# Attention in a two-stream encoder step: two PSUM banks used as halves, and a unit's output transposed two steps later

## The chip, the cores and the metric

The kernel runs on one core of one Trainium2 chip. The metric is the device time of one execution in microseconds. The core has five engines that run side by side, each its own queue in order: PE (TensorE, matrix products and transposes; its weight loads are listed as PEld), DVE (VectorE), ACT (ScalarE), POOL (GpSimd) and SP (SyncE, which here issues the DMAs). Products land in PSUM, which is eight banks of 128 partitions x 512 float32 values; DVE and ACT read them out from there into SBUF.

## The reference

One layer of an encoder is computed for 1024 prompt frames and for 64 new frames of a running stream that has a cache of 512 frames. All data are float32.

```python
z = einsum('btd,de->bte', x, w_in)      # one projection, its columns split among three head groups
# A: forgetting attention, 6 heads x 64, causal
s = q @ k.T / 8 + c_q - c_k              # c = cumsum(log f)
o_fox = softmax(where(kpos <= qpos, s, -1e30)) @ v
# B: chunked gating, 4 groups x 64: u * (tril(w_s) @ layer_norm(gelu(v)) + b_s) within 128 positions
# C: stick-breaking attention, 6 heads x 64, strictly causal
a = sigmoid(z) * prod over s < j < t of (1 - sigmoid(z_tj));  o_sb = a @ v
o = per-head RMSNorm([o_fox, o_sgu, o_sb]) * g_mix @ w_out
x = layer_norm(ALPHA * x + o);  x = layer_norm(ALPHA * x + square(relu(x @ w_up)) @ w_down)
```

The outputs are the new x of both streams and the new rows of keys, values, log forget gates and normalised gate rows.

## The kernel before

To keep float32 accuracy, an operand is split into a high and a low part, and a product is made of several passes over them (`PASSES`). A usual pair of instructions is thus an ACT copy that rounds to the high part and a DVE or POOL subtraction (`lo_sub`, line 98) that leaves the low part.

The kernel has three phases. Up to about 600 us: projections, attention and gating. Then, to about 700 us, the output projection ("mix") and the first LayerNorm. Then the MLP, whose products are on lines 1290 and 1748. Only the first phase is touched.

In the first phase two streams of work are written out one step at a time by a loop (lines 1092 to 1138): `fill()` makes the projections, whose products are on lines 360 and 501, in blocks of eight matmuls, and `attn()` does attention. The loop takes the next step from the stream that is behind by an estimate of its cost. This gives the order of the program. A planner then simulates the program on its own times and writes out each engine's queue; an instruction that comes later in the program can pass one whose inputs, in the simulation, are not ready. On the chip each queue runs in the written order.

Attention goes through six pairs of heads (three of A, then three of C). A pair has eight units and a sample unit. A unit is a block of 256 queries (u = 0 to 3) of one head (h = 0, 1). Its `a_steps` make two half rows of scores (line 559) and weights. Its `b_steps` use the weights in u + 2 steps: `tr` transposes up to four 128x128 blocks of them on PE (L607) into a bank "pt", from which ACT (L575) and DVE (L98) make the high and low part `pth`; `av` multiplies these with the values in four matmuls (L617 and L618 with the high part, L619 and L620 with the low part) into a bank "o", the sums over keys. In the last step ACT copies "o" to `osb` (L630), an SBUF tile with one buffer. The former unit's `c_step` then transposes `osb` on PE (L638, twice) into a bank "tr", DVE adds the two halves of the products into `ot` (L639), also one buffer, and after the second head of a block SP stores `ot` to HBM (L643). The sample unit makes its sums in "o" as well (L739, L743), and DVE takes them out straight into a new `ot` (L746), which has to wait for the store of the one before.

The bank "tr" has two other users: the keys of a projection are transposed there (`finish`, L484) and so are the cached keys of the sample (L676); both are taken out by `k_stack` with two ACT copies (L446) and two DVE subtractions.

PSUM is divided by tag: "acc", "s" and "pt" have two banks each, "o" and "tr" one each. A tile of "o" or "tr" is 256 columns wide, half of a bank, and each unit opens a new tile (`bufs=1`).

`attn()` interleaves the steps of the unit at hand (`b`) with the `a_steps` of the next (`nxt`), by turns, the next unit's first. A counter `k` counts the steps; after the second the pending `c_step` of the former unit is written out (line 1064). Where the next unit's queries are not projected yet, the unit at hand is first finished without counting.

## Time and profile before

| | |
|---|---|
| median of 3 runs | 1399.08 us (1395.83 to 1399.73) |
| profiled execution | 1399.96 us, its span 1398.2 us |
| mean granted TensorE clock | 0.983 |
| busy: PE, PEld, DVE, ACT, POOL | 1328.2, 1208.2, 1000.0, 720.2, 606.3 us |
| PE busy from 60 to 360 us, clock | 287.90 of 300 us, 0.99 |
| PE busy from 360 to 600 us, clock | 223.75 of 240 us, 0.95 |

In the profile a name such as `osbsb` is the tile's name without its numbers: "o" of a unit of pair "sb", and `osbsb` is also how `osb` of "sb" is shown; the line tells which is meant (L617 to L620 write the PSUM tile, L630 copies it into SBUF). `otpsb` is the tile in "tr". A row of a timeline has the start in us, the duration, the engine, line, operation, tile written <- tiles read, and in brackets how long the engine stood idle before it and for whom. A row of the waits has who waited for whom, the total in us, how often, and the longest.

### The profile page before, as it was taken

The page shows a single profiled execution, that of the slowest core. Times are in us where ns is not written, and L with a number is a line of the kernel's source. Part 1 is how long each engine was busy: PE and PEld are TensorE (multiplying, and loading weights), DVE is VectorE, ACT ScalarE, POOL GpSimd, SP SyncE. Part 2 cuts the span into 40 slices and gives each one's busy share as a digit, 9 for nine tenths or more (in the row PEclk, how much of TensorE's full clock was granted, in tenths as well). Part 3 has the DMA queues.
Part 4 walks back from the last instruction along what each step waited for, and adds up shares of the span by engine and source line. Part 5 has one row for each costly group of instructions (what it writes and reads, how often), then busy time and mean ns, then how long its engine had stood idle before and what let it go on. Part 6 is the DMA issues. An engine that isn't in the chain of part 4 may idle for free.

```text
span 1398.2 us, 24326 instructions
## 1 busy us (share of the span) xinstructions
PE 1328.2 (95%) x8827; PEld 1208.2 (86%) x8827; DVE 1000.0 (72%) x1795; ACT 720.2 (52%) x1561; POOL 606.3 (43%) x667
## 2 busy tenths in 40 slices
PE   7999999999898998999989999999998999999996
PEld 6899989999888987866889999999986788887875
DVE  3577666577788379787776687787668677767777
ACT  4366566566556366333432332322256677667675
POOL 3222222256665436755421222122156765565657
PEclk9999999999999999999999999999999999999999
DMA  7445564231403257432223444443468244444343
GB/s 219 91 130 157 156 203 122 65 80 43 106 16 72 64 161 252 150 112 68 76 85 118 167 140 131 155 140 122 169 232 309 91 169 141 145 136 154 99 135 128
DMA packets 159088, 185.64 MB, mean 133 GB/s; under 512 B 27756, under 2 KB 117164, under 8 KB 158968
## 3 DMA queue, kind: packets, MB, share of 16 engines
q1 hardware_dynamic: 158968, 184.08, 41.7%
q8 instruction: 70, 1.15, 0.3%
q14 instruction: 50, 0.41, 0.1%
HBM read 117.65 MB, written 60.10 MB: 127 GB/s over the span
## 4 chain that ended last, share of the span: by engine, by line
PE 65%; DVE 11%; DMA 8%; ACT 6%; POOL 5%; issue 4%; SPq 1%; DVEq 0%; ACTq 0%; POOLq 0%
PE zA L1290 9%; PE A L1748 8%; PE mx L249 7%; PE zD L1290 6%; PE kvsb L360 5%; PE D L1748 4%; PE zC L1290 3%; PE zB L1290 3%; PE kvfox L360 3%; PE B L1748 2%; DMA rwo<-w_out 2%; POOL wd L98 1%; PE qsb L501 1%; DVE snsb L543 1%; DMA xr<-x_prompt 1%
## 5 line engine op out<-in xcount | busy, mean ns | idle before, releaser
L98 POOL TENSOR_TENSOR wa<-wr,wa 128x512 fp32r<-128x512 f32 x42 | 62.8, 1521 | 227.0 <-ACT wa L1230 227.0
L98 POOL TENSOR_TENSOR wd<-rd,wd 128x512 fp32r<-128x512 f32 x77 | 100.3, 1314 | 107.9 <-ACT wd L1230 103.6
L249 PE MATMUL mx<-xT,oTb 128*128 128x512 f32 (+1 forms) x416 | 108.1, 412 | 1.0 <-ACT oTb L207 0.9
L1290 PE MATMUL zD<-xo,ws 128*128 128x288 f32 (+1 forms) x720 | 98.0, 289 | 1.9 <-DVE h4a L1454 1.6
L1290 PE MATMUL zA<-xo,ws 128*128 128x288 f32 (+1 forms) x720 | 98.0, 290 | 0.0
L249 PEld LDWEIGHTS mx<-xT,oTb 128*128 128x128 f32 (+1 forms) x416 | 78.7, 194 | 20.3 <-ACT oTb L207 1.4
L1290 PEld LDWEIGHTS zD<-xo,ws 128*128 128x128 f32 x720 | 93.6, 189 | 2.4 <-DVE h4a L1454 1.8
L1290 PEld LDWEIGHTS zA<-xo,ws 128*128 128x128 f32 x720 | 94.2, 190 | 0.0
L360 PE MATMUL kvfox<-wkvfox,xT 128*128 128x256 f32 (+3 forms) x624 | 90.2, 293 | 3.2 <-DVE fx L463 2.1
L1422 POOL TENSOR_TENSOR rd<-rd 128x512 f32<-128x512 f32 x56 | 79.3, 1417 | 29.3 <-DVE b L98 27.0
L545 POOL TENSOR_TENSOR sgsb<-sgsb,snsb 128x127 f32<-128x127 f32 (+7 forms) x48 | 58.4, 1217 | 75.8 <-DVE snsb L543 67.0
L360 PE MATMUL kvsb<-wkvsb,xT 128*128 128x256 f32 (+1 forms) x624 | 88.4, 287 | 0.0
L1230 ACT ACTIVATE wd<-rd 128x512 fp32r<-128x512 f32 x105 | 63.5, 623 | 45.1 <-POOL rd L1422 23.4
L1748 PE MATMUL A<-wd,wd 128*128 128x512 f32 x312 | 83.3, 396 | 3.3 <-DVE acc L1715 2.3
L360 PEld LDWEIGHTS kvfox<-wkvfox,xT 128*128 128x128 f32 (+1 forms) x624 | 81.3, 192 | 4.9 <-DVE fx L463 2.4
L543 DVE TENSOR_TENSOR_SCAN snsb<-snsb,one 128x128 f32<-128x128 f32 (+7 forms) x48 | 72.5, 1514 | 15.4 <-ACT snsb L542 14.7
L360 PEld LDWEIGHTS kvsb<-wkvsb,xT 128*128 128x128 f32 (+1 forms) x624 | 79.5, 187 | 0.2
L1301 ACT ACTIVATE sn<-zA 128x256 f32<-128x256 f32 (+1 forms) x80 | 30.9, 389 | 91.8 <-PE zA L1290 72.9
L1748 PEld LDWEIGHTS A<-wd,wd 128*128 128x128 f32 x312 | 58.1, 188 | 19.3 <-DVE acc L1715 3.6
L1748 PE MATMUL A<-wd,h4a 128*128 128x512 f32 x240 | 64.5, 394 | 0.6 <-DVE acc L1715 0.4
L1508 ACT ACTIVATE ws<-wr 128x1024 fp32r<-128x1024 f32 x28 | 29.0, 1056 | 57.4 <-DVE wr L1240 57.4
L1748 PEld LDWEIGHTS A<-wd,h4a 128*128 128x128 f32 x240 | 44.7, 188 | 12.2 <-ACT wd L1230 0.8
(548 smaller groups left out, 3754.5 us busy)
## 6 DMA issues: line engine op xcount, KB each, us to landing
h_dr<-hh SPq DMA_DIRECT2D x30, 512.0 KB, 3.2
rd<-w_down SPq DMA_DIRECT2D x30, 512.0 KB, 4.3
wr<-w_up SPq DMA_DIRECT2D x13, 1024.0 KB, 5.5
hr<-h_dr SPq DMA_DIRECT2D x31, 384.0 KB, 4.7
h_dr<-hh SPq DMA_DIRECT2D x30, 384.0 KB, 4.1
raw<-w_in SPq DMA_DIRECT2D x44, 256.0 KB, 3.4
wo_dr<-swo SPq DMA_DIRECT2D x32, 256.0 KB, 2.6
xT<-wo_dr SPq DMA_DIRECT2D x8, 1024.0 KB, 7.8
```

Of the source, the lines that this page charges most:

```text
L98: eng.tensor_tensor(out, src, hi.bitcast(F32), op=ALU.subtract)
L249: nc.tensor.matmul(acc[0:m], oT[:, k, hx, 0:m], wo[k // 4][hw][:, k % 4, cs], start=(i == 0), stop=(i == len(seq) - 1))
L360: nc.tensor.matmul(acc[0:n, c0:c0 + n1 - n0], xT[k // 4][:, k % 4, c:c + n], wt[:, k, hw, n0:n1], start=(i == 0), stop=(i == len(seq) - 1))
L501: nc.tensor.matmul(acc[:, 0:w], wq[:, k, hw, :], xT[k // 4][:, k % 4, c:c + w], start=(i == 0), stop=(i == len(seq) - 1))
L543: nc.vector.tensor_tensor_scan(g[:, 0:n][:, ::-1], g[:, 0:n][:, ::-1], one.broadcast_to([P, n]), 1.0, op0=ALU.mult, op1=ALU.bypass)
L545: nc.gpsimd.tensor_tensor(s[:, 0:n - 1], s[:, 0:n - 1], g[:, 1:n], op=ALU.mult)
L1230: nc.scalar.activation(hi, raw, AF.Copy)
L1290: nc.tensor.matmul(z, w[:, hw, k], xop(s, bo, hx)[:, k, :], start=(new and k == 0 and j == 0), stop=(k == 3 and j == 2), skip_group_check= ...
L1301: nc.scalar.activation(c, z, AF.Copy)
L1422: eng.tensor_tensor(r[:, o], r[:, x], r[:, y], op=ALU.subtract)
L1508: nc.scalar.activation(ws[:, 0, q, c], src[:, q], AF.Copy)
L1748: nc.tensor.matmul(z, h[:, hx, q, o], wset[self.c % 2][q][:, hw, wb], start=((n in (0, 3) or n == 1 and self.c == 0) and q == 0 and j == 0 ...
```

## The change

The tags "o" and "tr" now have one tile each, 512 columns wide, which is opened at the first use and kept for the phase. A function `half_bank` hands out its two halves by turns: each unit or transposition gets the half that the one before did not get. The pending `c_step` is written out after the fourth step of the interleaving, or at the unit's end if it has fewer; before, it was after the second step, and otherwise stayed pending.

```diff
+        halves = {}
+
+        def half_bank(tag):
+            if tag not in halves:
+                halves[tag] = [ps.tile([P, 512], F32, name=f"{tag}2", tag=tag, bufs=1), 0]
+            b, k = halves[tag]
+            halves[tag][1] = 1 - k
+            return b[:, k * 256:(k + 1) * 256]
...
-                pk = ps.tile([P, 2 * P], F32, name=f"pk{j}_{tiles[0]}", tag="tr", bufs=1)
+                pk = half_bank("tr")
...
-                o = ps.tile([P, 256], F32, name=f"o{nm}", tag="o", bufs=1)
+                o = half_bank("o")
...
-                    otp = ps.tile([P, 2, P], F32, name=f"otp{nm}", tag="tr", bufs=1)
+                    otp = half_bank("tr").rearrange("p (a b) -> p a b", a=2)
...
-                    pk = ps.tile([P, 256], F32, name=f"pkc{nm}_{m}", tag="tr", bufs=1)
+                    pk = half_bank("tr")
...
-                o = ps.tile([P, 256], F32, name=f"os{nm}", tag="o", bufs=1)
+                o = half_bank("o")
...
+            def turn():
+                while c_pend:
+                    c_pend.pop(0)()
...
-                    if k == 2 and c_pend:
-                        while c_pend:
-                            c_pend.pop(0)()
+                    if k == 4:
+                        turn()
+                turn()
                 settle(x)
-            while c_pend:
-                c_pend.pop(0)()
+            turn()
```

## The prediction

> **What bounds the kernel now.** I read the page first (span, busy shares), then the busy times by stretch, then who waited for whom on PE during attention, and then the order of single instructions around those waits.

> ```profile
> span 1398.2 us, 24326 instructions
> PE 1328.2 (95%) x8827; PEld 1208.2 (86%) x8827; DVE 1000.0 (72%) x1795; ACT 720.2 (52%) x1561; POOL 606.3 (43%) x667
> 360.00:600.00 240.00, 223.75 (x1594) 208.65 (x1594) 181.04 (x317) 129.84 (x325) 135.53 (x167) 0.95 0.39 115
> 380.00:384.00 4.00, 2.69 (x13) 2.71 (x14) 3.42 (x10) 2.61 (x10) 3.03 (x8) 0.69 0.45 116
> 444.00:448.00 4.00, 2.95 (x14) 2.66 (x13) 2.61 (x7) 2.97 (x7) 2.38 (x4) 0.50 0.35 82
> 552.00:556.00 4.00, 3.41 (x14) 3.12 (x15) 3.94 (x10) 1.74 (x4) 3.53 (x3) 0.52 0.96 309
> ```

> The stretch rows give start and end, length, busy time of PE, PEld, DVE, ACT and POOL, then TensorE's granted clock. TensorE is the bound: 95% of the span. The changed code is used only in the attention phase, up to about 600 us; what follows uses the same banks in the old way, so I expect it only to move in time. From 360 to 600 us PE is idle for 240 - 223.75 = 16 us and its clock is 0.95. Three stretches of 4 us have most of the low clock. So a gain or loss must come from PE's idle time in attention, and from the clock that it loses there.

> ```profile
> PE osb L619 <- DVE pthsb L98: 5.4, 9, 1.7
> PE otpsb L638 <- ACT osbsb L630: 5.0, 4, 1.7
> PE osb L617 <- ACT osbsb L630: 1.7, 1, 1.7
> PE pkcsb L676 <- DVE otsb L639: 0.8, 1, 0.8
> PE pksb L484 <- DVE kc_sb L98: 0.6, 1, 0.6
> PE ofox L617 <- ACT osbfox L630: 0.3, 1, 0.3
> PE otpfox L638 <- ACT osbfox L630: 0.2, 1, 0.2
> ```

> Each row is us in total, times, longest, from 60 to 580 us. Two edits aim at these rows. The waits on the bank of sums (L617 for L630) are 1.7 + 0.3 = 2.0 us, those on the bank of transposes (L676, L484) 0.8 + 0.6 = 1.4 us, and the late transposes (L638) wait 5.0 + 0.2 = 5.2 us. Together 8.6 us, or 0.6% of the time: that is the most that the waits named can give back directly.

> **The change, part by part.** *Halves.* "o" and "tr" become one tile each, of a full bank, of which successive users take columns 0-255 and 256-511 by turns. This helps only if a write to one half need not wait for the reader of the other. The kernel already has such halves: the chunk mixing (L803 to L810) puts two groups into the two halves of one bank.

> ```profile
> 412.91 0.45 PE L806 MATMUL sgm<-vh,wst 128*128 128x256 f32 x2
> 414.65 0.46 ACT L810 ACTIVATE so<-sgm,bs 128x256 f32<-128x256 f32 x1
> 415.16 0.51 PE L806 MATMUL sgm<-vh,wst 128*128 128x256 f32 x2 [0.62 <-ACT so L810]
> 419.95 0.47 ACT L810 ACTIVATE so<-sgm,bs 128x256 f32<-128x256 f32 x1
> 420.48 0.50 PE L806 MATMUL sgm<-vh,wst 128*128 128x256 f32 x2 [0.17 <-ACT so L810]
> ```

> The rows are start, duration, engine and line. The second group (415.16) needs nothing that ACT wrote, opens no new tile, and writes columns that ACT does not read; still PE stood 0.62 us until ACT's read of the first half ended (414.65 + 0.46 = 415.11). The fourth group does the same, 0.06 us after 420.42. So in this program halves of one tile are kept apart by a wait as if they were one buffer. I cost the halves at 0. The bounds: no worse than 0 by the copies themselves, and at best the 2.0 + 1.4 = 3.4 us of the rows above. I take 0, since the sgm rows are the same situation: PE write, ACT read, one bank.

> [...]

> *The later transposes.* Nothing is added or dropped: per unit two L638 transposes on PE, one L639 reduction on DVE, and for each second head one store (L643) on SP's queue, all emitted after the fourth step of the interleaving, not the second. What stands behind L638 on PE now?

> ```profile
> 353.78 0.44 PE L638 MATMUL otpsb<-ident,osbsb 128*128 128x128 f32 x2 [0.83 <-ACT osbsb L630]
> 353.98 0.37 PE L617 MATMUL osb<-pthsb,vpsb 128*128 128x256 f32 x1
> 380.86 0.38 ACT L630 ACTIVATE osbsb<-osb 128x256 f32<-128x256 f32 x1
> 381.19 0.69 DVE L98 TENSOR_TENSOR pthsb<-ptsb,pthsb 128x512 fp32r<-128x512 f32 x1
> 381.31 0.53 PE L638 MATMUL otpsb<-ident,osbsb 128*128 128x128 f32 x2 [1.73 <-ACT osbsb L630]
> 381.49 0.56 PE L617 MATMUL osb<-pthsb,vpsb 128*128 128x256 f32 x1
> 382.06 0.46 PE L619 MATMUL osb<-pthsb,vpsb 128*128 128x256 f32 x1
> 446.37 0.69 DVE L98 TENSOR_TENSOR pthsb<-ptsb,pthsb 128x512 fp32r<-128x512 f32 x1
> 446.67 0.69 PE L638 MATMUL otpsb<-ident,osbsb 128*128 128x128 f32 x2 [1.05 <-ACT osbsb L630]
> 447.01 0.56 PE L617 MATMUL osb<-pthsb,vpsb 128*128 128x256 f32 x1
> 447.58 0.41 PE L619 MATMUL osb<-pthsb,vpsb 128*128 128x256 f32 x1
> 550.57 0.44 PE L638 MATMUL otpsb<-ident,osbsb 128*128 128x128 f32 x2 [1.41 <-ACT osbsb L630]
> 551.06 0.39 PE L617 MATMUL osb<-pthsb,vpsb 128*128 128x256 f32 x1
> 552.24 0.58 PE L619 MATMUL osb<-pthsb,vpsb 128*128 128x256 f32 x1 [0.68 <-DVE pthsb L98]
> ```

> At all four long waits the next instruction is L617, the first product of the next unit. It opens the bank of sums, so it needs the same copy L630 that L638 waited for. With L638 later the 5.2 us vanish from its row and turn up at L617: -5.2 + 5.2 = 0. And if the halves did come apart, L619 would be late next, since it needs DVE's low part: at 381 that ends at 381.88, 0.18 us before L619 ran; at 446 at 447.06, 0.52 us before; at 552 L619 waited for it anyway. That would return 0.7 us in these three, not 4.2.

> *What the later step holds up.* The copy buffer osb is single. In the second unit of each pair's first block (u = 0, h = 1; six of them) the unit has only two steps, so its copy L630 is now emitted before the transposes that empty osb, and ACT must wait for them. The queue behind it on ACT holds the L575 copies that PE's L617 needs.

> ```profile
>   PE otpfox L638: 1.3, 1
> L360 PE MATMUL kvsb<-wkvsb,xT 128*128 128x256 f32 (+1 forms) x624 | 88.4, 287 | 0.0
> 369.23 0.41 DVE L639 TENSOR_REDUCE otsb<-otpsb 128x128 f32<-128x256 f32 x1
> 371.89 0.56 DVE L746 TENSOR_REDUCE otssb<-ossb 64x64 f32<-64x128 f32 x2
> 374.45 0.29 PE L617 MATMUL osb<-pthsb,vpsb 128*128 128x256 f32 x1
> SPq L643 <- DVE otsb L639: 49.2, 8, 19.3
> ```

> The first row is ACT's wait at L630 for L638 before the change: once, 1.3 us. Bounds: 0 (a wait that only is added gives nothing back) to 6 x 1.3 = 7.8 us. I take one more such wait, rounded to 1.0 us, since the single row is one in 48 copies. The sample unit has a like chain: L639, the store, then L746, which frees the sums for the next pair. The step is later by one block of eight fill matmuls, 8 x 88.4/624 = 1.1 us, and a half row of S, about 0.3 us by the same rate: 1.4 us. Between the end of L746 (372.45) and L617 (374.45) lie 2.0 us, so I cost it at 0; with one more block, 2.5 us, it would cost 0.5 us in each of six pairs, 3 us, the upper bound. On SP's queue the store moves behind perhaps one load; SP already stands 49.2 us before L643, so 0.

> **The sum.** The profiled execution took 1399.96 us, 1.8 us more than its span; the median of the runs shown is 1399.08, 0.9 lower. 1399.96 + 0 (halves) + 0 (L638's wait passed on) + 1.0 (osb) + 0 (sample) = 1401.0, less 0.9 is 1400.1 as a median. I say 1400.0. The measurement tells a difference from none at about 0.3%, 4.2 us.

> **The rivals.** *The change doesn't do what it says* is my forecast itself: the halves stay chained.

> *Faster: the stalls and their slow clock go.* The order on PE is written out by a planner from its own times. With L638 out of the front, it may put fill matmuls (L360) where PE now stands at 353, 381, 446 and 550. That gives 5.2 us, and the three stretches at 0.69, 0.50 and 0.52 lost 4 x (0.31 + 0.50 + 0.48) = 5.2 us of clock: 1400.0 - 10.4 = 1389.6. For it: the stalls sit right at or before those stretches. Against it: L617 needs the same copy. [...]

> *Slower: osb holds ACT.* Place: the six units named. Price: six waits of 1.3 us that reach PE through the L575 copies, 1399.1 + 7.8 = 1406.9. It decides from 0.7 us each (6 x 0.7 = 4.2). For it: ACT is in order, and PE has waits for ACT all through the phase. Against it: one wait in 48 so far. With the sample's 3 us the case reaches 1410.

> **How the numbers follow.** Forecast (within 4.2 us) 0.42: both main terms come out at zero by rows. Slower 0.34: both unpriced waits only add. Faster 0.24: it needs a new order to use the gap. The range 1388 to 1410 reaches to both rivals' ends (1389.6 less the 1.4 us of the tr waits; 1410) and leaves out about 0.15; the forecast's own range is 1396 to 1404.

> **What would show it.** Right: L638's wait for L630 under 1 us, L617's wait for L630 up from 2.0 to some 5 to 7 us; no L617 of a new unit before the end of the former unit's L630; from 700 us on, the same durations; clock 0.94 to 0.96 from 360 to 600 us. The slower rival: ACT's idle before L630 <- PE L638 of 5 us or more. The faster one: PE idle from 360 to 600 us under 11 us and clock 0.97 or more. Wrong at the root: an L617 that starts while L630 still reads the other half.

## The result and the profile after

| | before | after |
|---|---|---|
| median | 1399.37 us (1395.83 to 1399.73, 4 runs) | 1408.32 us (1407.26 to 1409.39, 4 runs) |
| ratio | | 1.0065 (95%: 1.0045 to 1.0086) |
| profiled execution, its span | 1399.96, 1398.2 us | 1407.26, 1405.5 us |
| first product of zA (MLP) to its last | 715.2 to 1033.3 us | 721.3 to 1039.5 us |

The changed kernel is 9.0 us slower, 0.65%. Lines of the attention code are numbered 10 higher than before (L638 is L648, L617 is L627 and so on), and the tiles `o…` and `otp…` are now `o` and `tr`. From the page of the changed kernel, the span and the busy times; then PE and the other engines by stretch, with the granted clock behind the five busy times:

```profile
span 1405.5 us, 24358 instructions
PE 1331.4 (95%) x8827; PEld 1209.2 (86%) x8827; DVE 994.2 (71%) x1795; ACT 720.3 (51%) x1561; POOL 611.8 (44%) x667
```

```profile
60.00:360.00 300.00, 287.72 (x2295) 278.63 (x2293) 196.31 (x475) 178.58 (x441) 96.85 (x156) 0.97 0.42 117
360.00:600.00 240.00, 216.92 (x1592) 201.71 (x1591) 176.09 (x308) 130.72 (x329) 135.37 (x165) 0.97 0.40 119
```

The work is the same (8827 matmuls), and the MLP takes the same time (318.2 us for zA, 318.1 before). So most of the time was lost before: zA starts 6.1 of the 7.3 us later that the span is longer; the other 1.1 us come after its last product. From 360 to 600 us PE is idle for 240 - 216.92 = 23 us, where it was 16. The clock is 0.97 in both stretches, where it was 0.99 and 0.95: lower in the first one, higher in the second. Over the whole execution it is 0.983 in both profiles, so between these two the 7.3 us are not slow clock; PE's idle time from 60 to 600 us is 7.0 us longer (28.4 and 35.4 us).

What PE waited for from 60 to 580 us, in the changed kernel (total us, times, longest):

```profile
PE o L629 <- DVE pthsb L98: 7.3, 8, 2.1
PE ptsb L617 <- DVE pthsb L98: 3.9, 2, 2.1
PE o L627 <- ACT pthfox L585: 3.3, 3, 1.8
...
PE o L627 <- ACT osbfox L640: 1.8, 2, 1.6
PE tr L648 <- ACT osbsb L640: 1.5, 1, 1.5
...
PE o L627 <- ACT pthsb L585: 1.1, 3, 0.6
...
PE tr L494 <- DVE otfox L649: 0.8, 1, 0.8
...
PE tr L494 <- DVE otsb L649: 0.6, 1, 0.6
...
PE tr L648 <- DVE otsb L649: 0.4, 1, 0.4
...
PE o L627 <- ACT osbsb L640: 0.2, 1, 0.2
...
PE o L629 <- DVE pthfox L98: 0.2, 1, 0.2
```

The late transposes (now L648) wait 1.5 us for the copy, no longer 5.2. But the waits on the bank of sums are still 1.8 + 0.2 = 2.0 us. In the pairs "sb", the low part from DVE is now waited for by the sums (L629) for 7.3 us instead of 5.4, and by the transposes of the weights (L617) for 3.9 us; before, there was no such row in these pairs. In all, PE's waits from 60 to 720 us grew from 35.7 to 40.7 us (sums of the rows).

Behind the span stands the clock as well. For each run I take span times mean granted clock as the time at full clock, and the rest as what slow clock cost. This is an estimate: it counts the slow stretches as if PE had set the pace all through them. I use this split below, as a mean over all runs of a kernel beside the runs of the kernel before on the same chip; the full-clock time has a standard error of 0.4 to 1.7 us, the difference in slow clock some 1 to 2 us.

### The profile page after: what moved, and what is told of

Its sections match the earlier page's. It is cut to its first block, busy times and chain, and to the rows that moved or that the text cites. A ratio compares the mean times of both kernels' runs of the same rounds, so it can differ in the third digit from the quotient of the medians.

```text
span 1405.5 us, 24358 instructions
## 1 busy us (share of the span) xinstructions
PE 1331.4 (95%) x8827; PEld 1209.2 (86%) x8827; DVE 994.2 (71%) x1795; ACT 720.3 (51%) x1561; POOL 611.8 (44%) x667
## 4 chain that ended last, share of the span: by engine, by line
PE 48%; DVE 12%; ACT 6%; POOL 5%; DMA 4%; issue 4%; SPq 0%; DVEq 0%; ACTq 0%; POOLq 0%
PE zA L1303 9%; PE A L1761 7%; PE zD L1303 6%; PE mx L249 5%; PE D L1761 3%; PE zC L1303 3%; PE kvsb L370 3%; PE zB L1303 3%; DVE snsb L553 2%; PE B L1761 2%; POOL wd L98 1%; DMA rd<-w_down 1%; DMA awa<-h_dr 1%; PE qsb L511 1%; DVE xo L98 1%
## 5 line engine op out<-in xcount | busy, mean ns | idle before, releaser
L98 POOL TENSOR_TENSOR wa<-wr,wa 128x512 fp32r<-128x512 f32 x42 | 63.8, 1546 | 227.1 <-ACT wa L1243 227.1
L98 POOL TENSOR_TENSOR wd<-rd,wd 128x512 fp32r<-128x512 f32 x77 | 100.9, 1322 | 106.3 <-ACT wd L1243 106.1
L1761 PEld LDWEIGHTS A<-wd,wd 128*128 128x128 f32 x312 | 58.1, 188 | 19.3 <-DVE acc L1728 3.6
```

What stands on the lines that cost most here:

```text
L98: eng.tensor_tensor(out, src, hi.bitcast(F32), op=ALU.subtract)
L1761: nc.tensor.matmul(z, h[:, hx, q, o], wset[self.c % 2][q][:, hw, wb], start=((n in (0, 3) or n == 1 and self.c == 0) and q == 0 and j == 0 ...
```

## The experiments

| kernel | step of the transposes | median, us | ratio to before (95%) | full-clock time, us (before) | lost to slow clock, us (before) |
|---|---|---|---|---|---|
| halves alone | 2 | 1396.52 | 0.9992 (0.9980 to 1.0004) | 1376.0 (1375.1) | 18.8 (20.8) |
| later alone | 4 | 1406.86 | 1.0064 (1.0045 to 1.0083) | 1380.3 (1375.1) | 24.8 (20.8) |
| changed, two osb | 4 | 1411.50 | 1.0097 (1.0080 to 1.0114) | 1382.1 (1375.1) | 27.6 (20.8) |
| changed, two ot | 4 | 1404.55 | 1.0042 (1.0026 to 1.0059) | 1380.6 (1375.1) | 21.7 (20.8) |
| before, step 1 | 1 | 1409.78 | 1.0095 (1.0064 to 1.0126) | 1382.4 (1375.7) | 26.8 (20.3) |
| before, step 3 | 3 | 1404.41 | 1.0037 (1.0016 to 1.0059) | 1379.3 (1375.7) | 22.0 (20.3) |
| before, step 6 | 6 | 1413.34 | 1.0111 (1.0089 to 1.0133) | 1388.0 (1375.7) | 23.6 (20.3) |
| before, w_out later | 2 | 1398.27 | 1.0003 (0.9989 to 1.0017) | 1376.3 (1375.7) | 19.9 (20.3) |
| before, weight 1.18 | 2 | 1395.62 | 0.9998 (0.9985 to 1.0011) | 1374.1 (1375.6) | 20.7 (19.9) |
| changed, weight 1.18 | 4 | 1398.57 | 1.0015 (0.9999 to 1.0031) | 1375.2 (1375.6) | 21.8 (19.9) |
| changed, w_out later | 4 | 1407.99 | 1.0084 (1.0062 to 1.0105) | 1380.6 (1375.6) | 25.0 (19.9) |
| before, two osb and ot | 2 | 1402.85 | 1.0052 (1.0033 to 1.0072) | 1380.5 (1375.6) | 21.3 (19.9) |

**Which of the two edits.** The halves alone:

```diff
-                o = ps.tile([P, 256], F32, name=f"o{nm}", tag="o", bufs=1)
+                o = half_bank("o")
...
-                    otp = ps.tile([P, 2, P], F32, name=f"otp{nm}", tag="tr", bufs=1)
+                    otp = half_bank("tr").rearrange("p (a b) -> p a b", a=2)
```

> The halves alone, the transposes after the second step as before. The instructions of this kernel stand in the same order on every engine as in the kernel before; only the addresses in the two banks differ. Theory A (the loss of 9 us comes from the later step, which leaves the copy of a unit's output and its transposes late, so that the next unit's sums wait): 1399 us, within 0.2% of before, kvsb at its first start at 222 us, granted clock 1.00 from 180 to 240 us. Theory B (the two halves cost time themselves, since writes and reads now meet in one bank): 1404 us or more, and the clock already low from 180 to 240 us. Theory C (the loss is a draw of the newly written order, whichever part made it new): 1399 us, as in A, because the order is the old one.

The later step alone, with the old tiles:

```diff
-                    if k == 2 and c_pend:
+                    if k == 4 and c_pend:
...
-                settle(x)
+                [c_pend.pop(0)() for _ in range(len(c_pend))]; settle(x)
```

> The later transposes alone, with the old tiles of 256 columns, one buffer each. The instructions stand in the same order on every engine as in the changed kernel. Theory A (later step): 1408 us, as the changed kernel, with the same stalls near 193 and 211 us. Theory B (halves cost): 1400 us. Theory C (a draw of the written order): 1408 us, as in A, because the order is that of the changed kernel. If the halves gain something that the later step hides, this kernel is slower than 1408 us.

The halves change nothing (0.9992) and the later step alone is the whole loss (1.0064, the changed kernel 1.0065). Theory B falls. In the traces the halves alone have the order of the kernel before on PE, ACT, DVE and POOL, and the later step alone that of the changed kernel. The rows of the halves alone, PE's waits and the place of the longest wait on the bank of sums:

```profile
PE o L619 <- DVE pthsb L98: 6.2, 9, 1.7
PE tr L638 <- ACT osbsb L630: 5.0, 4, 1.7
...
PE o L617 <- ACT osbsb L630: 1.5, 1, 1.5
```

```profile
302.10 0.38 ACT L630 ACTIVATE osbsb<-o 128x256 f32<-128x256 f32 x1
...
302.52 0.39 PE L617 MATMUL o<-pthsb,vpsb 128*128 128x256 f32 x1 [1.54 <-ACT osbsb L630]
```

These are the waits of the kernel before (5.4, 5.0, 1.7). At 302.10 ACT reads one half; the next unit's first product, into the other half, starts at 302.52, 0.04 us after the copy's end. For all 48 copies of this trace, no product for the sums starts during a copy. So in this program the halves are passed from user to user like one buffer.

**Does a single buffer hold the late transposes?** In the changed kernel ACT's copy stands at 194 us behind a pass of the w_out scaling that waited for its load, and PE stands behind the copy:

```profile
189.89 0.74 PE L569 MATMUL Sfox<-kpfox,qdfox 128*128 128x256 f32 x4 [1.24 <-DVE mfox L541]
...
193.71 0.72 ACT L989 ACTIVATE swo<-rwo,gmx 128x512 fp32r<-128x512 f32 x1 [2.17 <-DMA rwo<-w_out]
194.34 0.36 ACT L640 ACTIVATE osbfox<-o 128x256 f32<-128x256 f32 x1
...
194.76 0.49 PE L627 MATMUL o<-pthfox,vpfox 128*128 128x256 f32 x1 [1.58 <-ACT osbfox L640]
```

I took this for the price of the single `osb`, which the former unit's transposes had emptied only at 191 us. Two kernels give the changed one a second buffer, and one moves the w_out pass away:

```diff
-                osb = sa.tile([P, 256], F32, name=f"osb{nm}", tag="osb", bufs=1)
+                osb = sa.tile([P, 256], F32, name=f"osb{nm}", tag="osb", bufs=2)
```

> The changed kernel with two buffers for the copy of a unit's output (osb) in place of one, so that ACT's copy of the next unit need not wait until TensorE has transposed the former one. Theory A in the form 'the single osb holds the copies': the stall near 193 us goes, and with it the half clock behind it, so some 4 to 5 us of the 9 come back: 1403 to 1404 us. In the form 'both single buffers, osb and ot, hold': the same here, and the rest only with ot as well. Theory C (a draw of the order): the order is a new one again from unit (1,0) of the second pair on, and the time may come out anywhere from 1397 to 1409 us, without the stalls of 1.6 to 1.8 us following the transposes.

```diff
-                        st["ot"] = sa.tile([P, 2, P], F32, name=f"ot{nm}", tag="ot", bufs=1)
+                        st["ot"] = sa.tile([P, 2, P], F32, name=f"ot{nm}", tag="ot", bufs=2)
...
-                ot = sa.tile([P, 2, P], F32, name=f"ots{nm}", tag="ot", bufs=1)
+                ot = sa.tile([P, 2, P], F32, name=f"ots{nm}", tag="ot", bufs=2)
```

> The changed kernel with two buffers for the reduced transposes (ot) in place of one, so that DVE's reduction need not wait for the store of the former unit. Theory A with ot as the holder: the wait of 2.89 us of the reduction near 212 us goes, and the half clock from 212 to 220 us with it, 3 to 4 us back: 1404 to 1405 us; the stall near 193 us stays. If osb alone is the holder: 1408 us. Theory C (a draw of the order): anywhere from 1397 to 1409 us, the place of the stalls having no relation to ot.

```diff
-    WO_FROM = 44
+    WO_FROM = 52
```

> The changed kernel with the scaling of w_out begun after 52 steps of the filling work in place of 44. In the changed kernel the copy of a unit's output stood on ACT at 194 us behind a pass of this scaling that waited 2.17 us for its load. Theory A in the form 'the copy waits behind that pass': the stall at 194 us goes, 1.6 to 3.3 us back, 1405 to 1407 us. Theory A in the general form: 1404 to 1410 us. Theory C: anywhere from 1396 to 1410 us.

With two `osb` the wait on the copy near 194 us is gone, and the kernel is slower still (1.0097). New waits stand in its place; from its waits, 60 to 590 us:

```profile
PE Sfox L569 <- DVE mfox L541: 3.7, 3, 3.2
PE kvsb L370 <- ACT kvssb L471: 3.5, 1, 3.5
```

Moving the w_out pass gives nothing back (1.0084). So theory A falls in the forms "`osb` holds the copy" and "that pass holds the copy": each edit makes the planner write another order, the one stall goes, and others come. For `ot` it stays open. With two `ot` no reduction waits for the store any more, there is no slow clock at 212 us (1.00 from 198 to 226 us), and 1404.55 us is what this form expected. But the profile of the later step alone has no slow clock at that place either (1.00 from 192 to 216 us), the ratio (1.0026 to 1.0059) overlaps with that of the later step alone (1.0045 to 1.0083), the full-clock time is the same (1380.6 and 1380.3 us), and the order is a new one here too.

**Does each step of delay cost?** The kernel before with the transposes after another step, which is the diff of the later step alone with 1, 3 or 6 in place of 4. These kernels also write out what is pending at the unit's end. That needs no control of its own: with the step left at 2 it gives the program of the kernel before, instruction for instruction.

> The kernel before, with the pending transposes after the first step in place of the second (and at the unit's end if there are fewer). Theory A (each step of delay costs, since the copy and its transposes come later): at least as fast as before, 1395 to 1397 us, and no wait of the next unit for DVE's or ACT's copies that before does not have; or a little slower, if the transposes now wait for the copy of the sums (5 us of such waits in before, up to 8). Theory C (a draw of the written order, no trend in the step): anywhere from 1393 to 1408 us.

> The kernel before, with the pending transposes after the third step. Theory A: between the kernel before and the changed one, 1400 to 1403 us. Theory C: anywhere from 1393 to 1408 us, with no place on a line between the second and the fourth step.

> The kernel before, with the pending transposes after the sixth step, or at the unit's end. Theory A: slower than the changed kernel by some 4 to 9 us, 1411 to 1416 us, since a delay of four steps costs twice that of two. Theory C: anywhere from 1395 to 1410 us. If the time is that of the changed kernel: most units have no more than four steps of their own, or the cost is that of one event only.

Steps 3, 4 and 6 cost 0.37, 0.64 and 1.11%, in this order as theory A has it. But step 1 costs 0.95%: earlier is no better. Waits at the late transposes don't explain that. PE's waits with step 1, then with step 6, 60 to 580 us:

```profile
PE ofox L617 <- ACT pthfox L575: 4.6, 2, 3.2
...
PE sgv L360 <- DVE sgvv L759: 3.7, 3, 1.6
...
PE otpsb L638 <- ACT osbsb L630: 2.5, 2, 1.8
```

```profile
PE osb L619 <- DVE pthsb L98: 9.8, 8, 3.2
PE ofox L617 <- ACT pthfox L575: 3.5, 2, 2.1
```

With step 1 the longest waits are at the sums and at the gating's projection, which are no waits for the transposes or their copies; with step 6 the sums wait for DVE's low part for 9.8 us.

**Is it the step, or the newly written order?** Three kernels write a new order with the step left at 2 (the w_out scaling begun later, with the diff above; another weight in the interleaving; two buffers each for `osb` and `ot`), and one puts the other weight into the changed kernel.

```diff
-        RATIO, LEAD = (1.2,) * 4 + (1.2, 1.3), 6
+        RATIO, LEAD = (1.18,) * 4 + (1.2, 1.3), 6
```

> The kernel before, with the scaling of w_out (its loads, the ACT and DVE passes and the stores) begun after 52 steps of the filling work in place of 44; the transposes stay after the second step. This edit is not about the transposes; it only makes the order on the engines a new one, from the second pair on. Theory A: 1396 to 1399 us, as before, within 0.2%. Theory C (any new order draws a new set of stalls, and before is a lucky one): several us off before, more likely slower: 1400 to 1406 us.

> The kernel before with the attention's costs in the interleaving weighed by 1.18 in place of 1.2 for the first four pairs; the transposes stay after the second step. About 1400 of the 8829 TensorE instructions stand elsewhere in its order, somewhat fewer than between the kernel before and the changed one (2170). Theory A (the step of the transposes sets the cost): within 0.3% of before, 1394 to 1401 us. Theory C (any newly written order draws its own stalls, and the order before is a lucky one): 1401 to 1410 us.

> The changed kernel with the same other weight, 1.18. About 2000 TensorE instructions stand elsewhere than in the changed kernel. Theory A: some 5 to 12 us slower than the kernel before with the weight 1.18, 1402 to 1410 us. Theory C: no fixed distance to it; as likely below 1400 us as above 1408.

> The kernel before (whole banks, transposes after the second step) with two buffers each for the copy of a unit's output (osb) and for the reduced transposes (ot). Theory A: the waits for these buffers go and nothing else changes in the step, 1393 to 1398 us. Theory C: a new order as different from before as the changed kernel's (some 2400 TensorE instructions stand elsewhere), so 1400 to 1410 us; and then more buffers are no help with the transposes after the fourth step either.

Neither theory holds as it was put. Two of the new orders with step 2 cost nothing (1.0003 and 0.9998), against theory C. They are milder, though: by line, operation and shape, PE's order in the traces differs from the kernel before at 598 and 996 of 8827 places, with the later step at 1434. Nor does the number of places decide: the changed kernel with the weight 1.18 differs at 1908. But two more buffers at step 2 cost 0.52%, against theory A, and with the weight 1.18 the later step is only 0.17% slower than step 2 with the same weight (1.0015 by 0.9998), less than can be measured here. So it is shown that the later step makes the 9 us with the weight of this kernel, and that with a slightly different one it costs at most some 0.4% (the 0.17% with its uncertainty): how much it costs depends on the order that the planner writes around it. That the step costs nothing by itself is not shown; steps 3, 4 and 6 do rise in order. The split says the same: with the weight 1.2 the later step costs 5.2 us of full-clock time and 4.0 us of slow clock (standard error 1.7), with 1.18 it costs 1.1 and 1.1 us.

What stays open is which property of the order decides. PE's waits don't tell it: with the weight 1.18 and step 4 their longest rows from 60 to 580 us are much like those of the changed kernel.

```profile
PE o L629 <- DVE pthsb L98: 6.6, 6, 2.3
PE o L627 <- ACT pthfox L585: 3.8, 3, 2.1
...
PE ptsb L617 <- DVE pthsb L98: 2.2, 1, 2.2
PE tr L648 <- DVE kc_sb L98: 2.0, 1, 2.0
```

All waits from 60 to 720 us sum to 43.6 us there and to 40.7 us in the changed kernel, whose profiled span is 8 us longer (1405.5 and 1397.5 us). None of the twelve kernels beats the kernel before by what can be measured.

## Why the prediction was right or wrong

**Halves, 0.** Right, with its reason: the halves alone give 0.9992, and the waits are the old ones. That no product into one half starts while ACT reads the other was one of the marks named, and it held in all 48 copies. A product that starts during such a read is in no run, so what it would give is not shown.

**Later transposes, -5.2 + 5.2 = 0.** This is the step that failed. The first half held: L638's wait fell from 5.2 to 1.5 us (forecast: under 1). The second did not go where I sent it. L617's wait for the copy stayed at 2.0 us (forecast: up to 5 to 7); what grew is the wait for DVE's low part (L619 and L607, together 5.4 + 0.7 + 0.4 = 6.5 us before, 7.3 + 0.2 + 3.9 = 11.4 after) and for ACT's high part (L617: 1.7 + 0.5 before, 1.1 + 3.3 after). The wait of 381 us shows how. Before, a row of ACT ahead of the copy at 380.86, which the prediction doesn't show:

```profile
380.74 0.22 ACT L515 ACTIVATE qssb<-qsb 128x64 f32<-128x64 f32 x1 [0.72 <-DVE qdsb L510]
```

Its counterpart in the changed kernel:

```profile
389.11 1.21 DVE L553 TENSOR_TENSOR_SCAN snsb<-snsb,one 128x512 f32<-128x512 f32 x1
...
389.61 0.39 PE L627 MATMUL o<-pthsb,vpsb 128*128 128x256 f32 x1 [0.20 <-ACT pthsb L585]
...
390.54 0.43 DVE L520 SCALAR_TENSOR_TENSOR qdsb<-qsb,qdsb 64x256 fp32r<-64x256 f32 x1
...
391.00 0.43 DVE L649 TENSOR_REDUCE otsb<-tr 128x128 f32<-128x256 f32 x1
...
391.45 1.16 DVE L98 TENSOR_TENSOR pthsb<-ptsb,pthsb 128x512 fp32r<-128x512 f32 x2
...
392.20 0.39 PE L629 MATMUL o<-pthsb,vpsb 128*128 128x256 f32 x1 [2.09 <-DVE pthsb L98]
```

The first product waits 0.20 us only, but two products later PE stands 2.09 us for the low part, which is behind the scan, a subtraction and the reduction L649 on DVE. Before, the same DVE queue had held up ACT (the 0.72 us above) and the copy behind it, and PE stood 1.73 us at L638. I had written that L619 would be late next, 0.18 us behind, but only for the case that the halves came apart; I looked at PE's next instruction and not at the queue at the root of the wait. The larger fault is that the sum prices the edit with the order of everything else kept. I named the planner only as a way to gain (the faster rival). That term of the sum was 0; measured, a new order was worth from nothing (1.0003, 0.9998) to 5.9 us (two osb and ot) with the step left alone, and the later step from 3.0 us, which is not clear of nothing, to 9.6 us depending on the order around it.

**osb, +1.0 us, and the slower rival.** Its figure, 1406.9 us, came near the 1408.3 measured, but its mechanism did not appear. ACT's wait for the transposes, expected at 5 us or more, in the changed kernel:

```profile
ACT osbfox L640 <- PE tr L648: 0.2, 1, 0.2
```

In the order as written only one of the 48 copies had to wait for transposes, and a second buffer made the kernel slower. The near hit is no support for that rival.

**Sample chain and SP's queue, 0.** The sample's part was right: no wait on its DVE pass (now L756) stands among PE's waits. For the store it was not: the prediction looked at SP's waits and not at the single `ot` behind it. DVE's reduction waited 1.3 us for the store in the kernel before (L639, longest 0.6), and 6.0 us in the changed one:

```profile
DVE otsb L649 <- DMA o_dr<-otsb: 3.1, 1, 3.1
DVE otfox L649 <- DMA o_dr<-otfox: 2.9, 1, 2.9
```

PE stands 0.83 us behind the second of them (the row of L494 for `otfox`); as told above, it stays open what these waits cost in all. The later part came nearly as forecast: 684.2 us from the first product of zA to the end, 683.0 before.

**The clock.** I expected 0.94 to 0.96 from 360 to 600 us; it was 0.97 there and fell to 0.97 from 60 to 360 us, where I had expected nothing. Slow clock was no term of my sum at all, and it is 4.0 of the 9.2 us by the split. The reading of the clock before was wrong too: the three stretches do not have most of the low clock from 360 to 600 us, but 5.2 of 240 x 0.05 = 12 us.

**The whole.** 1408.3 lies within 1388 to 1410 but outside the forecast's own range of 1396 to 1404; "slower", which was given 0.34, came true. That it lies within the wide range is luck: the range reached so high for the sake of `osb` and the sample chain, and neither appeared: ACT waited 0.2 us for the transposes, PE not at all for the sample's pass.

## What to carry to other kernels

Where a planner writes the order, moving one small step re-deals the whole order, so price that by trial: change something unrelated as well (a weight, a start) and see how far the time moves, before a gain or loss is put down to the edit. Follow a wait back to the queue at its root; here that queue stayed, and the wait moved to the next reader (L638's from 5.2 to 1.5 us, those for DVE's low part from 6.5 to 11.4). Two halves of one bank are one buffer as long as the program makes their users wait for each other: here that gave 0.9992, with a next product 0.04 us after the copy's end.

## What the runs showed of the hardware

| PE idle in the slot, us of 3.41 | slots | followed by a slot at 0.50 |
|---|---|---|
| below 1.2 | 2683 | 29, of which 28 were at 0.50 already |
| 1.2 to 1.8 | 98 | 36 |
| 1.8 and more | 75 | 75 |

In these counts it is not one long gap that goes with a slow slot, but the idle time within the slot before: in the kernel before, the slot from 620.42 us had 1.89 us of it with no gap longer than 0.71 us, and 6.83 us at 0.50 followed. A slow spell held more easily here than it started: of the slots at 0.50, all 27 with 0.7 us or more of idle time were followed by another slow one, and 7 of the other 113; at full clock, 0.7 to 1.2 us had that effect in 1 of 163. So one order can come out with different times. The later step alone has the same order as the changed kernel and nearly the same stalls near 190 and 210 us, but its profiled execution took 1403.89 us and the other 1407.26. The slots of the changed kernel, and then those of the later step alone, with length, five busy times and clock:

```profile
191.47:194.88 3.41, 1.78 (x11) 1.05 (x11) 2.29 (x7) 1.24 (x5) 0.00 (x0) 1.00 0.34 112
194.88:201.70 6.82, 6.82 (x32) 6.69 (x33) 2.90 (x6) 3.18 (x7) 0.00 (x0) 0.50 0.73 249
208.53:211.94 3.41, 1.52 (x11) 1.08 (x9) 0.78 (x2) 1.93 (x5) 1.05 (x1) 1.00 0.94 234
211.94:218.77 6.83, 6.09 (x28) 5.79 (x29) 3.96 (x8) 2.42 (x6) 1.50 (x2) 0.50 0.63 181
```

```profile
185.40:188.81 3.41, 2.04 (x16) 1.76 (x14) 2.99 (x8) 2.50 (x6) 0.00 (x0) 1.00 0.55 181
188.81:192.22 3.41, 2.35 (x15) 1.40 (x14) 2.53 (x7) 1.33 (x3) 0.00 (x0) 1.00 0.60 153
192.22:199.05 6.83, 5.94 (x45) 5.45 (x46) 4.67 (x10) 5.05 (x13) 0.74 (x3) 1.00 0.73 244
202.46:205.87 3.41, 2.53 (x22) 2.29 (x20) 1.54 (x3) 1.72 (x4) 1.35 (x2) 1.00 0.65 183
205.87:209.28 3.41, 2.63 (x21) 2.39 (x22) 2.94 (x6) 2.83 (x8) 1.28 (x1) 1.00 0.82 219
```

In the first, PE is idle for 3.41 - 1.78 = 1.63 and 1.89 us in one slot, and 6.8 us at half clock follow each time, by estimate at a price of up to 6.8 x 0.5 = 3.4 us each. In the second, the grid falls otherwise. The stall near 190 us is there in this row:

```profile
192.69 0.39 PE L617 MATMUL ofox<-pthfox,vpfox 128*128 128x256 f32 x1 [1.49 <-ACT osbfox L630]
```

The slot that ends at 192.22 has 1.06 us of idle time, and the last 0.47 us of the stall fall into the next; the other stall falls into the slots with 0.88 and 0.78 us. The clock stays at 1.00.
